# Layer 0's value projection moved out of the attention and into one stretch of seven half-size products

## The chip, the cores and the metric

The kernel runs on one core of a Trainium2 chip. The metric is the device time of one execution in microseconds. Of the kernel before, three runs were timed: 2423.89, 2424.85 and 2425.2 us, median 2424.85.

## What is computed

A decoder trunk of two layers on 1024 positions of width 1024, all in float32. Layer 0 is differential attention with 8 head pairs, layer 1 forgetting attention with 16 heads; each is followed by a gated MLP. Residuals go through a LayerNorm. What matters here is the beginning of layer 0:

```python
q, k, v = jnp.split(x @ w_qkv, 3, axis=-1)          # three 1024x1024x1024 products
q = apply_rotary(q.reshape(B, S, H, 2, d), cos, sin, PARTIAL_ROT)
k = apply_rotary(k.reshape(B, S, H, 2, d), cos, sin, PARTIAL_ROT)
v = v.reshape(B, S, H, 2 * d)
s = jnp.einsum('bhcqd,bhckd->bhcqk', qb, k) * scale
p = masked_softmax(s, causal_mask(start, Q_BLOCK, S))
a = p[:, :, 0] - lam * p[:, :, 1]
o = jnp.einsum('bhqk,bhkd->bqhd', a, v)             # then RMS norm and the output product
```

## The kernel before, in words

Every float32 operand of a large product is held as two parts, a rounded high part and a low rest (`split`, L85: ScalarE makes the high part, VectorE the rest). A product is then three matmuls (`mm3`, L97): high by high, low by high, high by low. A "step" of a projection is one such triple, 128x128 stationary by 512 columns.

Layer 0's attention goes by 8 pairs of heads (`attention`, L853). A pair has 16 jobs: 8 blocks of 128 queries, two halves each. A job is its scores on TensorE (`scores`, L647: two matmuls per up to 512 keys), the mask and row minimum in one VectorE instruction (L664), the exponential with row sums on ScalarE (L687), a reciprocal and, for the first half, the scaling of the probabilities on VectorE (L690, L692), for the second half the difference of the two on VectorE (L697). Differences are transposed on TensorE (L1531), split from PSUM into `pt` (L88, L92) and multiplied with the values (L1554). Each of these comes one job after the one before, so that the engines overlap; each engine works through its instructions in order.

While a pair attends, TensorE also projects the next one: `project` (L554) is a generator whose steps are placed between the jobs. In layer 0 these are 48 steps, for three weight slabs (queries, keys, values) of 512 KB by two halves of the positions; `attention` spreads them by weights, query block number plus 1 plus `W_C`. Work that follows a step is queued by a count of steps (`after`, L295; `pulse`, L303): copying a result to SBUF (`result`, L592, after `D_EV`), collecting the rows that rotary turns with 12 small DMAs (`gather`, L612), turning them with three VectorE instructions and four DMAs back (`turn`, L625, after `D_ROT`), splitting queries and keys (`halves`, L604, after `D_CUT`). Values come out of their projection as 128 dimensions by 512 positions; four transposes (`turn_v`, L638) bring them into the layout for L1554, and they are split into two tiles. The next weight slabs are fetched by `ahead` and split by `ready`.

The first pair's projection runs ahead of all (`first_pair_rotary`, L336): queries and keys by halves of the positions, then its values, with the loads of x, its splits, the sine tables and the constants around it. The seven other pairs' values are made inside pairs 0 to 6.

Layer 1 makes the values of all pairs ahead of its attention in one stretch (`value_steps`, L445, run by `Steps`, L1571). It splits the 1024x1024x1024 product into halves in each dimension and computes seven half-size products in place of eight, in the order 1, 2, 5 and 6 alternating, 7, 4, 3. The operands are sums and differences of the quarters: `x1` and `x2` of the activations, `B` of the weights, made by accumulating DMAs on GpSimd's queue and by VectorE (`make`). Each product has 4 row blocks by 4 inner blocks by 3 matmuls, x stationary and weights moving, 512 columns wide; the results are gathered in `c12`, split and written to `vv` in DRAM, from where `load_values` (L549) brings a pair's two value tiles back.

Instructions marked by `keep_in_program_order` stay in the order in which the program issues them on their engine; others may be moved by the scheduler when the program is built. SyncE (SP) issues most DMAs and stops at one whose data or buffer isn't ready; GpSimd (POOL) issues the rotary tables' and the accumulating ones.

## Time and profile before

| | |
|---|---|
| median of three runs | 2424.85 us |
| the profiled execution | 2425.8 us, its span 2424.0 us |
| TensorE clock granted | 0.999 |
| TensorE busy | 2388.8 us (99%), 11691 matmuls |
| VectorE busy | 1921.5 us (79%) |
| ScalarE busy | 1323.3 us (55%) |
| GpSimd busy | 160.1 us (7%) |
| layer 0's eight pairs | from 48.3 to 488.5 us |
| layer 1's eight pairs | from 1308.1 to 1719.2 us |

Busy times are of the span. A matmul's duration in the profile holds its passage through the array, in which the next one already runs; so the sum of durations is more than the time that matmuls take, and the distance between two starts is the measure. A row of a group tells, after the bar, the group's busy time, the mean duration of one in ns, the idle time of the engine just before them and what ended most of it.

### The profile page before, as it was taken

The page shows a single profiled execution, that of the slowest core. Times are in us where ns is not written, and L with a number is a line of the kernel's source. Part 1 is how long each engine was busy: PE and PEld are TensorE (multiplying, and loading weights), DVE is VectorE, ACT ScalarE, POOL GpSimd, SP SyncE. Part 2 cuts the span into 40 slices and gives each one's busy share as a digit, 9 for nine tenths or more (in the row PEclk, how much of TensorE's full clock was granted, in tenths as well). Part 3 has the DMA queues.
Part 4 walks back from the last instruction along what each step waited for, and adds up shares of the span by engine and source line. Part 5 has one row for each costly group of instructions (what it writes and reads, how often), then busy time and mean ns, then how long its engine had stood idle before and what let it go on. Part 6 is the DMA issues. An engine that isn't in the chain of part 4 may idle for free.

```text
span 2424.0 us, 33635 instructions
## 1 busy us (share of the span) xinstructions
PE 2388.8 (99%) x11691; PEld 1991.6 (82%) x11691; DVE 1921.5 (79%) x3755; ACT 1323.3 (55%) x2504; POOL 160.1 (7%) x341
## 2 busy tenths in 40 slices
PE   8999999999999999999999999999999999999998
PEld 6888888878888888888777888888888888888886
DVE  5788888999766767887876888789898676678977
ACT  4666666656544444444545777776565444445444
POOL 2111111110000000000220111110010000000000
PEclk9999999999999999999999999999999999999999
DMA  6232323622322224964476323335222222239751
GB/s 176 73 85 83 87 78 97 206 96 79 105 79 79 79 95 130 351 229 155 150 171 197 89 80 92 102 102 186 87 97 87 79 87 95 79 100 334 260 170 70
DMA packets 144322, 307.51 MB, mean 127 GB/s; under 512 B 27452, under 2 KB 46908, under 8 KB 144152
## 3 DMA queue, kind: packets, MB, share of 16 engines
q1 hardware_dynamic: 140472, 298.22, 38.5%
q0 software_dynamic: 3680, 7.15, 1.5%
q8 instruction: 92, 1.51, 0.3%
q14 instruction: 78, 0.64, 0.1%
HBM read 196.83 MB, written 67.57 MB: 109 GB/s over the span
## 4 chain that ended last, share of the span: by engine, by line
PE 82%; DVE 9%; DMA 4%; ACT 3%; issue 1%; SPq 1%; DVEq 0%; POOL 0%; ACTq 0%; POOLq 0%
PE m L101 20%; PE m L103 19%; PE m L102 19%; PE s L101 4%; PE s L102 4%; PE s L103 4%; PE m L1531 3%; PE s L662 3%; PE s L661 2%; PE m L1557 1%; DVE wo L92 1%; PE m L1556 1%; DMA pt<-in_wd 1%; DMA wb<-in_wd 1%; DVE oa L92 1%
## 5 line engine op out<-in xcount | busy, mean ns | idle before, releaser
L101 PE MATMUL m<-xh,wh 128*128 128x512 f32 x640 | 268.2, 419 | 10.8 <-ACT xh L88 8.9
L101 PE MATMUL m<-xh,wo 128*128 128x512 f32 x656 | 255.4, 389 | 0.9 <-DVE xl L92 0.9
L102 PE MATMUL m<-xl,wo 128*128 128x512 f32 x656 | 255.2, 389 | 0.0
L103 PE MATMUL m<-xh,wo 128*128 128x512 f32 x656 | 255.2, 389 | 0.0
L103 PE MATMUL m<-xh,wl 128*128 128x512 f32 x640 | 253.9, 397 | 0.4 <-DVE wl L92 0.4
L102 PE MATMUL m<-xl,wh 128*128 128x512 f32 x640 | 252.8, 395 | 0.4 <-DVE xl L92 0.4
L88 ACT ACTIVATE wo<-wg 128x512 fp32r<-128x512 f32 x168 | 106.3, 633 | 222.7 <-PE m L103 215.1
L664 DVE CUSTOM_DVE_ANT_0 s<-s,mask 128x128 f32<-128x128 f32 (+7 forms) x256 | 194.4, 760 | 22.6 <-PE s L662 21.5
L101 PE MATMUL m<-q,wo 128*128 128x512 f32 x472 | 184.0, 390 | 0.0
L102 PE MATMUL m<-q,wo 128*128 128x512 f32 x472 | 183.6, 389 | 0.0
L103 PE MATMUL m<-q,wo 128*128 128x512 f32 x472 | 183.6, 389 | 0.0
L88 ACT ACTIVATE pt<-m 128x512 fp32r<-128x512 f32 (+1 forms) x240 | 129.4, 554 | 83.4 <-PE m L1531 67.2
L92 DVE TENSOR_TENSOR pt<-m,pt 128x512 fp32r<-128x512 f32 (+1 forms) x240 | 148.9, 633 | 15.5 <-ACT pt L88 12.8
L88 ACT ACTIVATE wo<-t 128x512 fp32r<-128x512 f32 x132 | 82.7, 627 | 140.6 <-PE m L103 131.2
L656 POOL CAST qz<-q 64x128 fp32r<-64x128 f32 x256 | 101.0, 397 | 766.8 <-PE s L662 672.5
L101 PEld LDWEIGHTS m<-xh,wh 128*128 128x128 f32 x640 | 121.6, 190 | 31.7 <-ACT xh L88 8.9
L92 DVE TENSOR_TENSOR wo<-wg,wo 128x512 fp32r<-128x512 f32 x168 | 115.3, 688 | 37.9 <-ACT wo L88 37.1
L101 PEld LDWEIGHTS m<-xh,wo 128*128 128x128 f32 x656 | 123.2, 188 | 27.0 <-PE m L1120 1.4
L103 PEld LDWEIGHTS m<-xh,wo 128*128 128x128 f32 x656 | 123.1, 188 | 25.6
L102 PEld LDWEIGHTS m<-xl,wo 128*128 128x128 f32 x656 | 123.1, 188 | 25.4
L103 PEld LDWEIGHTS m<-xh,wl 128*128 128x128 f32 x640 | 121.0, 189 | 27.3 <-DVE wl L92 1.4
L102 PEld LDWEIGHTS m<-xl,wh 128*128 128x128 f32 x640 | 122.0, 191 | 16.9 <-DVE xl L92 0.9
(404 smaller groups left out, 6311.1 us busy)
## 6 DMA issues: line engine op xcount, KB each, us to landing
t<-in_wi SPq DMA_DIRECT2D x44, 512.0 KB
ha<-ad SPq DMA_DIRECT2D x88, 256.0 KB
wg<-in_wi SPq DMA_DIRECT2D x42, 512.0 KB
ad<-t SPq DMA_DIRECT2D x42, 512.0 KB
wst<-in_w SPq DMA_DIRECT2D x38, 512.0 KB
q<-q SPq DMA_DIRECT2D x128, 128.0 KB
pt<-in_wd SPq DMA_DIRECT2D x24, 512.0 KB
hb<-in_wd SPq DMA_DIRECT2D x44, 256.0 KB
```

Of the source, the lines that this page charges most:

```text
L88: i = nc.scalar.activation(hi, src, AF.Copy, scale=1.0 if scale is None else scale)
L92: nc.vector.tensor_tensor(lo, src, hi.bitcast(F32), op=ALU.subtract)
L101: mm(out, wh, xh, start=start, stop=False)
L102: mm(out, wh, xl, start=False, stop=False)
L103: mm(out, wl, xh, start=False, stop=stop)
L656: nc.gpsimd.tensor_copy(qz[r:r + 64, :], q[r:r + 64, qt * P:qt * P + P])
L661: nc.tensor.matmul(sb[:, ks], q[:, qt * P:qt * P + P], kd[:, ks], start=True, stop=False)
L662: nc.tensor.matmul(sb[:, ks], qz[rows], kl[rows, ks], start=False, stop=True)
L664: nc.vector.tensor_tensor_reduce(sb[:, :ln], sb[:, :ln], self.mask[:, S - ln:], 1.0, BIG, ALU.add, ALU.min, mn)
L1531: nc.tensor.transpose(tb[:, w:w + P], self.pts[q][:, kt * P:kt * P + P], k.ident)
L1556: mm(o, self.v[0][:, vs], h, start=first, stop=False)
L1557: mm(o, self.v[0][:, vs], l, start=False, stop=last)
```

## The change

1. Layer 0's values. `project` keeps layer 1 alone. `first_pair_rotary` prepares sums of quarters of x and of the value weights, straight from DRAM (`xT`, `wv0`), by plain DMAs on SP and accumulating ones on GpSimd, and runs `value_steps` for all pairs, after the queries and keys of pair 0 and ahead of its attention. Slabs of values, `turn_v` and its transposes are gone. Pairs fetch their values with `load_values`, 10 steps into the pair before.
2. The projection in the pairs (`project_rotary`) has 32 steps, for queries and keys. All pairs' generators are chained; pair 0 takes 36 steps, pair 6 takes 28. `W_C` of layer 0 is 6 in place of 2.
3. Rotation: gather per operand (6 DMAs at a time), turn 7 steps after the last projection, cut 11 steps after it. For pair 0, turn, gather and cut are hung on the steps of the value stretch (`V_ROT`, `V_GA`, `V_CUT`). The gather buffer `rt` is one half tile for all; its other half holds probabilities of the second half for the first four query blocks.
4. The scaling of the first half's probabilities (L692) is on ScalarE. The sums of squares in `diff_values` come two steps after in place of one.
5. The sines and the load of the exponentials' table after them are pinned on ScalarE, ahead of the second half of x; lambda's exponential comes after the queries and keys of pair 0, pinned. Spare tiles come from other pools.
6. A pair's output is stored in two parts; output tiles that are fetched back come from another pool.

The diff, without some of the plain renamings (buffers picked by layer, names, imports):

```diff
 AHEAD = 6
 EARLY = 2
-D_EV, D_ROT, D_CUT, D_TV = 1, (9, 10), ((16, 16), (22, 24)), 1
+D_EV, D_ROT, D_CUT = 1, (7, 7), ((11, 11), (11, 11))
+V_ROT, V_GA, V_CUT = (20, 42), 19, (31, 54)
+SHIFT = 4
 W_CUT = 3
-D_V, D_VAL = (5, 9), 10
-LAG, VLAG, W_C = 1, 0, (2, 6)
+D_VAL = 10
+LAG, VLAG, W_C = 1, 0, (6, 6)
 FL = 1
 TR = ((0, 1), (2, 3, 4), (5, 6, 7), ())
 PIN = 1
...
-        d = self.cp.tile([P, 2], F32, name="lamd")
+        d = self.lamd = self.cp.tile([P, 2], F32, name="lamd")
-        nc.scalar.activation(d, d, AF.Exp)
+    def lam_exp(self):
+        nc, d = self.nc, self.lamd
+        self.tc.keep_in_program_order(nc.scalar.activation(d, d, AF.Exp))
...
     def rope_tables(self):
         nc, q = self.nc, self.nc.gpsimd
         ang, n, cos, sin = self.angles
-        nc.scalar.activation(cos, n, AF.Sin)
-        nc.scalar.activation(sin, ang, AF.Sin)
+        for d, a in ((cos, n), (sin, ang)):
+            self.tc.keep_in_program_order(nc.scalar.activation(d, a, AF.Sin))
+        self.tc.keep_in_program_order(nc.scalar.preload_act_table_set("natural_log_exp_and_others"))
...
-    def exp_table(self):
-        nc = self.nc
-        with self.tc.tile_critical(no_gpsimd_drain=True):
-            nc.scalar.preload_act_table_set("natural_log_exp_and_others")
-            for t in self.angles[2:]:
-                nc.scalar.copy(t[:, :1], t[:, :1])
...
                 self.load_x(0, (4 * n + 2 * s,))
         self.rope_tables()
         self.load_x(1)
-        self.w[2] = self.weight(self.slabs[2])
     def first_pair_rotary(self, t):
-        dst = [self.tmp() for s in range(3)]
+        H, lo, hi = KT // 2, slice(0, 512), slice(512, 1024)
+        dst = [self.tmp() for s in range(2)]
         self.xh, self.xl = {}, {}
         with self.tc.tile_critical(no_gpsimd_drain=True):
             self.nc.scalar.preload_act_table_set("trig_and_small")
         self.rope_angles()
         self.first_loads()
         self.consts()
-        r = {}
+        self.rt = self.lp.tile([P, 1024], F32, tag="lg", name="rt")
+        self.lam()
+        pool = self.nc.gpsimd.dma_start
+        sync = lambda *a: self.tc.keep_in_program_order(self.nc.sync.dma_start(*a))
+        x, wv, B = self.i["xT"], self.i["wv0"], {}
+        tiles = [self.qp.tile([P, 1024], F32, tag="q1", name=self.nm("vw")) for _ in range(7)] + [self.tmp()]
+        x1 = [self.tmp(pool=self.wp, tag="wst", bufs=2) for _ in range(2)] + \
+            [self.tmp(pool=self.tt, tag="pt") for _ in range(2)]
+        x2 = [y[:, ns] for y in (self.tmp(pool=self.tt, tag="pt"), self.tmp(pool=self.pp, tag="p")) for ns in (lo, hi)]
+        c12 = [self.tmp(pool=self.pp, tag="p") for _ in range(4)]
+        hold = t[5:7] + [self.tp.tile([P, 1024], F32R, tag="of", name=self.nm("vs"), bufs=1)]
+        def weights(c):
+            for r, ns in ((1, lo), (2, hi)):
+                for k in range(H):
+                    B[r, c, k] = tiles[4 * c - 4 + k][:, ns]
+                    sync(B[r, c, k], wv[r * H - H + k][:, c * 512 - 512:c * 512])
+        def sums(d, *terms):
+            sync(d, x[:, terms[0][0], terms[0][1]])
+            for kt, ns in terms[1:]:
+                pool(d, x[:, kt, ns], accum_op=ALU.add)
+        weights(1)
+        for k in range(H):
+            sums(x1[k][:, lo], (k, hi), (H + k, hi))
+            sums(x2[k], (k, hi), (H + k, hi), (k, lo))
+        weights(2)
+        for k in range(H):
+            sums(x1[k][:, hi], (k, lo), (k, hi))
+        steps = self.value_steps(0, B, x1, x2, lambda k: pool(x2[k], x[:, H + k, lo], accum_op=ALU.add), c12, hold)
+        r = {"t": self.rt}
         for c in range(2):
             ps = [self.mbank() for _ in range(2)]
             for _ in zip(*[self.dense_steps(ps[s], *self.w[s], c) for s in range(2)]):
                 pass
+            for s in range(2):
+                self.result(0, 0, s, c, ps[s], dst[s], t, True)
+        self.lam_exp()
+        for c in range(2):
+            for j in range(2):
+                self.after(V_ROT[c] - V_GA, self.gather, dst, r, c, j)
+            self.after(V_ROT[c], self.turn, dst, r, c)
+            for j in range(2):
+                self.after(V_CUT[c], self.halves, dst, t, c, j)
+        steps.run(4)
+        steps.drains()
+        steps.run(-4)
+        self.ahead(2)
+        steps.run(-2)
+        self.load_values(0, 0, t)
+        self.ahead(3)
+        self.ready(2)
+        steps.run(-1)
+        self.ready(3)
+        steps.run()
+    def project_rotary(self, p, t):
+        dst, r, i = [None] * 2, {"t": self.rt}, 2 * p
+        for n, (s, c) in enumerate(((0, 0), (1, 0), (0, 1), (1, 1))):
+            if n % 2:
+                self.ahead(i + 2 + n // 2)
+                self.after(5, self.ready, i + 2 + n // 2, True)
+            if p == NP - 1 and n > 1:
+                self.out_ahead(0, n - 2)
+            ps = self.mbank()
+            yield from self.dense_steps(ps, *self.w[i + s], c)
+            if c == 0:
+                dst[s] = self.tmp()
+            self.after(D_EV, self.result, 0, p, s, c, ps, dst[s], t)
+            self.after(D_EV + (5 if n == 0 else 1), self.gather, dst, r, c, s)
+            if s == 1:
+                self.after(D_ROT[c], self.turn, dst, r, c)
+                for j in range(2):
+                    self.after(D_CUT[c][j], self.halves, dst, t, c, j)
             if c:
...
+                del self.w[i + s]
     def first_pair(self, l, t):
...
     def project(self, l, p, t):
...
+        i = 2 * p
+        for n, (s, c) in enumerate([(s, c) for s in range(2) for c in range(2)]):
+            if n % 2:
                 self.ahead(i + 2 + n // 2)
             else:
                 self.after(W_CUT, self.ready, i + 1 + n // 2, True)
-            if s == 2 - l and p == NP - 1:
+            if s and p == NP - 1:
                 self.out_ahead(l, c)
             ps = self.mbank()
             yield from self.dense_steps(ps, *self.w[i + s], c)
...
+            self.after(D_EV, self.result, l, p, s, c, ps, None, t)
             if c:
                 del self.w[i + s]
...
         sl = slice(c * 512, c * 512 + 512)
         if dst is not None:
-            self.nc.scalar.activation(dst[:, sl], ps, AF.Copy, scale=-DH ** -0.5 if s == 0 else 1.0)
+            i = self.nc.scalar.activation(dst[:, sl], ps, AF.Copy, scale=-DH ** -0.5 if s == 0 else 1.0)
+            if pin:
+                self.tc.keep_in_program_order(i)
         elif s == 0:
             if c == 0:
                 self.qlo = self.tp.tile([P, 1024], F32R, tag="t", name=self.nm("ql"))
...
-    def gather(self, dst, r, c):
-        if "t" not in r:
-            r["t"] = self.tmp()
-        t = r["t"][:, c * 512:c * 512 + 512]
-        for j, x in enumerate(dst[:2]):
...
+    def gather(self, dst, r, c, j):
+        t = r["t"][:, :512]
+        x = dst[j]
+        for h in range(2):
+            rows = 64 * j + 32 * h
+            n = slice(c * 512 + h * 256, c * 512 + h * 256 + 256)
+            self.nc.sync.dma_start(t[rows:rows + 32, :256], x[48:80, n])
+            for y in range(2):
+                self.nc.sync.dma_start(t[rows + y:rows + 32:2, 256:], x[49 - y:80:2, n])
-        t = r["t"][:, c * 512:c * 512 + 512]
+        t = r["t"][:, :512]
...
-    def turn_v(self, g, vf, va, vb):
-        tb = self.mbank()
-        for j in range(4):
-            self.nc.tensor.transpose(tb[:, j * P:j * P + P],
-                                     vf[:, (4 * g + j) * P:(4 * g + j + 1) * P], self.ident)
-        gs = slice(g * 512, g * 512 + 512)
-        self.after(D_TV, self.split, va[:, gs], vb[:, gs], tb)
...
         sb, ln, mn = self.scores(0, t[j], t[2 + j], t[4], j, qt)
         lsum = self.small(tag="ls")
         yield
-        pt = self.tmp(pool=self.pp, tag="p") if j == 0 else self.tmp() if last and qt > 2 else \
+        pt = self.tmp(pool=self.pp, tag="p") if j == 0 else self.rt[:, 512:] if qt < 4 and not (last and qt % 2) else \
+            self.tmp() if last and qt > 2 else \
             self.tmp(pool=self.wp, tag="wst", bufs=2)
         nc.scalar.activation(pt[:, :ln], sb[:, :ln], AF.Exp, bias=mn, scale=-1.0, accum_out=lsum)
         yield
         rs = self.small(tag="rs")
         nc.vector.reciprocal(rs, lsum)
         if j == 0:
-            nc.vector.tensor_scalar(pt[:, :ln], pt[:, :ln], rs, None, op0=ALU.mult)
+            nc.scalar.activation(pt[:, :ln], pt[:, :ln], AF.Copy, scale=rs)
             pr["p"] = pt
         else:
             p0 = pr["p"][:, :ln]
...
             nc.tensor.matmul(ms, self.ones, lo, start=False, stop=True)
             done.append(True)
-        self.after(1, sums)
+        self.after(2, sums)
         yield
         while not done:
             yield
...
         self.od = self.dr.tile([NP, P, 1024], F32, name=f"od{l}")
         tiles = lambda p: [self.qtile((p + l) % 2) for _ in range(7)] + \
             ([self.lp.tile([P, 1024], F32R, tag="lg", name=self.nm("kb"))] if l else [])
-        self.wo = NP * (3 - l)
-        self.slabs = [self.i[f"w{l}"][s * NP + p] for p in range(NP) for s in range(3 - l)]
+        self.wo = NP * 2
+        self.slabs = [self.i[f"w{l}"][s * NP + p] for p in range(NP) for s in range(2)]
         self.slabs += [self.i[f"wo{l}"][k] for k in range(8)]
         self.w, self.stage, self.queue = {}, {}, []
         self.ofs = {}
...
         cur = tiles(0)
         self.first_pair(l, cur) if l else self.first_pair_rotary(cur)
         live, values = [], []
+        tl = [[] for _ in range(NP)]
+        early = chain(*[self.project_rotary(p, tl[p]) for p in range(1, NP)])
         for p in range(NP):
-            nxt = tiles(p + 1) if p < NP - 1 else None
-            if nxt is not None:
-                self.fill, n = self.project(l, p + 1, nxt), 48 - 16 * l
-                if l:
-                    self.after(D_VAL, self.load_values, l, p + 1, nxt)
+            nxt = None
+            if p < NP - 1:
+                nxt = tiles(p + 1)
+                if l == 0:
+                    tl[p + 1] += nxt
+                    self.fill, n = early, 32 + SHIFT * ((p == 0) - (p == NP - 2))
+                else:
+                    self.fill, n = self.project(l, p + 1, nxt), 32
+                self.after(D_VAL, self.load_values, l, p + 1, nxt)
             else:
                 self.fill, n = self.out_early(l), 64
             jobs = (self.diff_jobs if l == 0 else self.fox_jobs)(p, cur)
...
             while done < n:
                 self.step()
                 done += 1
-            next(self.fill, None)
+            if l or p > NP - 3:
+                next(self.fill, None)
             cur = nxt
         self.fill, n = self.out_late(l), 12
         while live or values:
...
             self.fetch_o(l, 0)
             self.after(8, self.load_o, 0, None, (0,))
         else:
-            if l:
-                self.after(6, self.ready, self.wo + 1, True)
+            self.after(6, self.ready, self.wo + 1, True)
             self.after(3, self.load_o, 0, None, (1,))
             self.after(4, self.fetch_o, l, 1)
             self.after(8, self.load_o, 1)
...
     def finish(self):
         if self.end is not None and next(self.end, True):
             self.over = True
-            if self.last and self.p < NP - 1:
+            if self.l == 0 and self.c4 == 2 and self.p < NP - 1:
+                self.k.nc.sync.dma_start(self.k.od[self.p][:, :768], self.k.ofs[self.p][:, :768])
+            elif self.l == 0 and self.last and self.p < NP - 1:
+                self.k.nc.sync.dma_start(self.k.od[self.p][:, 768:], self.k.ofs.pop(self.p)[:, 768:])
+            elif self.last and self.p < NP - 1:
                 self.k.nc.sync.dma_start(self.k.od[self.p], self.k.ofs.pop(self.p))
```

83 lines of the change are left out of this document (17 added, 66 removed).

## The prediction

> **What bounds the kernel now.** I read the busy shares first, then the stretches of layer 0's attention one by one, then single instructions.
>
> ```profile
> span 2424.0 us, 33635 instructions
> PE 2388.8 (99%) x11691; PEld 1991.6 (82%) x11691; DVE 1921.5 (79%) x3755; ACT 1323.3 (55%) x2504; POOL 160.1 (7%) x341
> ```
>
> TensorE is busy nearly throughout. In the view by stretches the columns are length, then busy time and count for PE, PEld, DVE, ACT and POOL, the granted clock, the DMA share and GB/s. I cut at the first score product of each pair: the row from 48.30 is pair 0, 98.20 pair 1, 265.30 pair 4, 375.20 pair 6, 430.00 pair 7 (which carries the output projection). 1452.70 is a pair of layer 1, and 1208.90 is layer 1's own value stretch with what is mixed into it.
>
> ```profile
> 8.90:24.30 15.40, 14.77 (x47) 10.88 (x48) 12.67 (x28) 8.98 (x19) 5.28 (x10) 1.00 0.92 294
> ...
> 48.30:98.20 49.90, 48.27 (x246) 39.69 (x246) 40.07 (x101) 28.51 (x64) 5.80 (x16) 1.00 0.36 95
> 98.20:154.30 56.10, 55.19 (x305) 47.09 (x304) 47.18 (x118) 36.74 (x83) 5.51 (x16) 1.00 0.32 90
> ...
> 265.30:320.30 55.00, 55.00 (x306) 47.08 (x305) 46.04 (x114) 35.89 (x81) 7.06 (x16) 1.00 0.30 82
> ...
> 375.20:430.00 54.80, 54.80 (x306) 47.06 (x304) 47.00 (x112) 38.38 (x86) 7.19 (x16) 1.00 0.40 110
> 430.00:488.50 58.50, 57.29 (x305) 48.09 (x303) 56.23 (x130) 34.21 (x79) 6.05 (x15) 1.00 0.57 195
> ...
> 1452.70:1502.10 49.40, 49.12 (x298) 42.69 (x297) 40.68 (x107) 35.60 (x74) 6.03 (x16) 1.00 0.33 92
> 1208.90:1308.00 99.10, 98.66 (x444) 77.92 (x443) 73.96 (x129) 48.65 (x90) 15.17 (x18) 1.00 0.74 177
> ```
>
> A pair takes 55.0 us with TensorE never idle, VectorE busy for 46.04 and ScalarE for 35.89. So layer 0's attention is TensorE's, and VectorE has 55.00 - 46.04 = 9.0 us to spare in a pair. That reserve is what this change spends.
>
> A matmul's busy time isn't its price, since matmuls overlap. The starts tell the pitch:
>
> ```profile
> 24.73 0.39 PE L101 MATMUL m<-xh,wh 128*128 128x512 f32 x1
> ...
> 25.86 0.39 PE L103 MATMUL m<-xh,wl 128*128 128x512 f32 x1
> ...
> 279.08 0.60 PE L642 MATMUL m<-ident,t 128*128 128x128 f32 x4
> 279.44 0.48 PE L101 MATMUL m<-xh,wh 128*128 128x512 f32 x1
> ```
>
> Between the first two rows lie five steps (four rows between are left out): 1.13 / 5 = 0.227 us for a 512-wide matmul. Four transposes take 279.44 - 279.08 = 0.36 us, 0.09 each.
>
> **The change part by part.** *Removed from TensorE.* A slab is 2 x 8 x 3 = 48 matmuls. These groups over 0 to 470 us hold the 24 slabs of queries, keys and values, and the values' transposes:
>
> ```profile
> L101 PE MATMUL m<-xh,wh 128*128 128x512 f32 x384 | 159.0, 414 | 9.2 <-ACT xh L88 8.9 <-ACT wh L88 0.2
> ...
> L642 PE MATMUL m<-ident,t 128*128 128x128 f32 x64 | 10.1, 277 | 0.9 <-DVE pt L92 0.9
> ```
>
> 3 x 384 = 24 x 48, and a third of it is values: 384 matmuls x 0.227 = 87.2 us. 64 transposes x 0.09 = 5.8 us. Together -93.0.
>
> *Added to TensorE.* Seven products of 4 x 4 x 3 = 48 matmuls, all 512 wide: 336 x 0.227 = +76.3. The net is -16.7 us if TensorE waits nowhere more than now. All value work leaves the pairs: each loses 10.9 + 0.7 = 11.6 us, so a pair like that of 265.30 would be 43.4 us (pair 0 keeps four steps more and pair 6 four fewer, which cancel), and 76.3 us come in ahead of them.
>
> *Entry into the stretch.* Today the values' matmuls follow the last query/key matmul directly, on a weight split long before. Now ScalarE copies both results in pinned order, does the pinned exponential of lambda and only then splits the first value weight:
>
> ```profile
> 35.12 1.28 ACT L596 ACTIVATE t<-m 128x512 f32<-128x512 f32 x2 [2.35 <-PE m L103]
> 37.68 0.20 ACT L165 ACTIVATE lamd<-lamd 128x2 f32<-128x2 f32 x1 [1.28 <-DVE lamd L164]
> ```
>
> 1.28 + 0.20 and a 512-wide split of 0.6 (rather more than half the 1.06 of a 1024-wide one, shown below): TensorE stands for about 2.0 us near 35 us. Lower bound 0, if the copies come earlier; upper 4, if the weights land late. I take 2.0, as nothing else in the order can fill it.
>
> Such a hole can also cost clock. In layer 1 two waits close together were followed by matmuls at half pace:
>
> ```profile
> 1314.11 0.47 PE L662 MATMUL s<-q,qz 66*128 66x128 f32 x2 [1.50 <-DMA q<-cd]
> 1315.86 0.33 PE L661 MATMUL s<-q,q 128*128 128x128 f32 x1 [1.28 <-ACT p L835]
> ...
> 1317.70 0.54 PE L101 MATMUL m<-xh,wh 128*128 128x512 f32 x1
> ...
> 1319.64 0.63 PE L661 MATMUL s<-q,q 128*128 128x512 f32 x1
> 1320.07 0.63 PE L662 MATMUL s<-q,qz 66*128 66x512 f32 x1
> ...
> 1321.41 0.39 PE L101 MATMUL m<-xh,wh 128*128 128x512 f32 x1
> ```
>
> 0.43 us from 1319.64 to 1320.07 is nearly double 0.227, over some 3.7 us from 1317.70 to 1321.41: half of that, 1.8 us, is lost. Between 0 and 1.8 I take 0.9, since one hole of 2.0 is shorter than those two together (2.8).
>
> The Trainium skill (TensorE: Matmul & The Clock Gate, What's actually happening) says that the array falls to half rate only after a whole idle window of about 3.4 us, free-running. By that rule the 2.0 us hole costs no clock and the sum is 0.9 us lower; the rows above fell with 2.8 us of visible waits and two short products between them, so the rule doesn't settle it.
>
> *The stretch itself.* Layer 1's own stretch runs with TensorE busy 98.66 of 99.10 us and VectorE at 75%: 0.4 us of visible waits. Layer 0 takes its sums from accumulating DMAs on POOL's queue, 20 of them, and each second term waits for the first to land:
>
> ```profile
> pt<-xl POOLq DMA_DIRECT2D x6, 256.0 KB, 5.0
> ```
>
> ```profile
> 27.01 1.03 POOL L220 DMA_DIRECT2D rope<-rs  x2 [4.69 <-DMA rs<-sp]
> ```
>
> At 5.0 us a landing (a median, layer 1) plus issues of about half a microsecond (1.03 for two), a step k needs 6 to 7 us, the four of them 24 to 28. POOL is in the rotation tables' DMAs until 28 us; so the sums are done by 52 to 56, and the fifth product, their first reader, starts near 35 + 2 + 2 x 10.9 = 59. The bytes that products 5 and 6 need are 16 weight quarters and 20 terms of sums of 256 KB, 9 MB; at the 294 GB/s of the first row (0.92 share) they take 31 us from about 24, done by 55. Both fit, narrowly; I add 0.5, with bounds 0 and 10.
>
> *The pairs.* VectorE and ScalarE lose and gain these (pair 4, then the same scaling on ScalarE in layer 1):
>
> ```profile
> L92 DVE TENSOR_TENSOR wl<-wst,wh 128x1024 fp32r<-128x1024 f32 x3 | 3.7, 1224 | 0.6 <-ACT wh L88 0.5
> ...
> L692 DVE TENSOR_SCALAR p<-p,rs 128x128 f32<-128x128 f32 (+7 forms) x8 | 4.2, 519 | 0.2
> L690 DVE RECIPROCAL rs<-ls 128x1 f32<-128x1 f32 x16 | 2.4, 158 | 4.9 <-ACT wst L687 2.8 <-ACT p L687 2.1
> ...
> L92 DVE TENSOR_TENSOR q<-m,q 128x512 fp32r<-128x512 f32 x2 | 1.4, 692 | 0.2
> ```
>
> ```profile
> L88 ACT ACTIVATE wh<-wst 128x1024 fp32r<-128x1024 f32 x3 | 3.2, 1057 | 0.0
> L596 ACT ACTIVATE t<-m 128x512 f32<-128x512 f32 x6 | 3.6, 596 | 2.3 <-PE m L103 2.2
> L88 ACT ACTIVATE q<-m 128x512 fp32r<-128x512 f32 x2 | 1.2, 599 | 0.9 <-PE m L642 0.9
> ...
> L842 ACT ACTIVATE p<-p,rs 128x128 f32<-128x128 f32 (+5 forms) x6 | 4.4, 728 | 0.8 <-DVE rs L838 0.8
> L842 ACT ACTIVATE t<-t,rs 128x512 f32<-128x512 f32 (+1 forms) x2 | 1.9, 938 | 0.3 <-DVE rs L838 0.2
> ```
>
> VectorE: 46.0 - 1.2 (one weight) - 4.2 (scaling of the first half's probabilities) - 1.4 (values) = 39.2, 90% of 43.4. ScalarE: 35.9 - 1.1 - 1.2 - 1.2 + 6.3 = 38.7, 89%. Three engines near 90% wait on each other in turn: score, minimum on VectorE, exponential on ScalarE, reciprocal on VectorE, scaling now on ScalarE. The best likeness is pair 7 of today: VectorE at 56.23 of 58.50, 96%, and TensorE idle for only 1.2 us. Layer 1's pair with VectorE at 82% loses 0.3. So a pair's waits lie between 0.3 and 1.2 by these rows, and above that if ScalarE's 89%, which no pair has today (at most 38.38 of 54.80), costs its own. I take 0.8 x 7 = +5.6. Later sums of squares (two steps instead of one) and the other spread of steps over the jobs work on these waits and are in that number.
>
> *Pair 7* loses VectorE's scaling too, some 4 of its 56 us; of its 1.2 us idle I take 0.7 back. *Handover into pair 0*: the last products' drains stand ahead of its first scores on both engines, +1.0 (pair 0 today: 49.90 - 48.27 = 1.6 idle already).
>
> *Costed at nothing.* These rows bear on it:
>
> ```profile
> L226 ACT ACT_TABLE_LOAD x1 | 1.3, 1283 | 3.9 <-DMA t<-t 3.9
> ```
>
> ```profile
> 19.13 1.16 ACT L88 ACTIVATE xh<-p 128x512 fp32r<-128x512 f32 x2 [1.49 <-DMA p<-in_xT]
> ...
> 36.35 2.44 SPq L636 DMA_DIRECT2D t<-t  x4
> ...
> 39.82 1.14 ACT L88 ACTIVATE q<-t 128x512 fp32r<-128x512 f32 x2
> ```
>
> The table load (1.28 us) moves ahead on ScalarE, to before the splits of the second half of x; there ScalarE stands 1.49 us for the load of x anyway, which hides it; without that cover it costs 1.3 once. Rotation: turn and cut come 4 steps apart, 4 x 43.4 / 32 = 5.4 us. From the first write-back's issue to the cut that reads it passed 39.82 - 36.35 = 3.5 us, and the three VectorE operations before it, of half the size of the 692 ns subtraction above, are under 2.1: it just fits. Without that cover ScalarE waits in order at the cut, twice a pair, and the exponentials queue behind it. The gathers are issued 6 at a time instead of 12. Two value loads replace one weight load on SP's queue, and the split output store is one issue more; DMA (share 0.30 in pair 4) has room for both.
>
> **Sum.** 2425.8 (the profiled execution; its span is 2424.0) - 16.7 + 2.0 + 0.9 + 0.5 + 5.6 - 0.7 + 1.0 = 2418.4. The median of the runs is 2424.85, 0.95 under the profiled one: 2417.5. Where today's pairs 0 to 2 lose more than the later ones (pair 1: 56.10 against 55.00), the spread of steps may give back some 1.5 us: I forecast **2416**.
>
> **The rivals.**
>
> *In-order chain (slower).* VectorE and ScalarE become the bound of the pairs. VectorE's 9.0 us idle in a pair is largely waiting (4.9 at the reciprocal alone). If this waiting doesn't shrink as the pair does, a pair takes 39.2 + 9.0 = 48.2. All else gives -16.7 + 3.4 + 0.3 - 1.5 = -14.5, or 2.1 a pair: the change turns into a loss once a pair exceeds 45.5, that is, once more than 6.3 of the 9.0 us stay. At 7.2 it is 46.4 and 7 x 3.0 - 14.5 = +6.5: **2431**. For it: ScalarE at 89%, and one more trip between the two engines per job. Against it: pair 7 leaves VectorE only 2.3 us.
>
> The Trainium skill (TensorE: Matmul & The Clock Gate, the table at its head) calls ScalarE's and VectorE's queues strict first-in-first-out, eight deep. That rule speaks for this rival, since whatever waits at the head holds the rest; the reciprocal's row above shows such a wait.
>
> *Starved stretch (no change).* Sums or weights land late, as POOL's chain takes 28 us or more beside saturated DMA: each of the first steps of products 5 and 6 waits 2 to 3 us, +9 in all with the lost clock: **2425**. For it: the narrow fit above. Against: the first reader is 24 us behind the start.
>
> *Nearly the whole gain.* The engines absorb all, the hole at the entry is short, pairs 1 and 7 recover: -16.7 + 2 - 3 = **2407**.
>
> *The rotation is too close (the pinning doesn't serve).* Each of 14 cuts holds ScalarE for 1.5 us, of which half reaches TensorE: +10, **2426**.
>
> **How the numbers follow.** Forecast 0.47 (its own range 2410 to 2421), nearly the whole gain 0.14, in-order chain 0.21, starved stretch 0.11, close rotation 0.07. Changes within 0.2% (4.85 us) can't be told from none here. Faster: 0.47 less its upper end (0.03), 0.14 and a little of the last two: 0.61. Slower: the chain's 0.21 less 0.03, and the tails of the last two, 0.03: 0.21. Same: 0.18. The range for 8 in 10 runs from 2404 (all of the gain and 4 back) to 2433 (a pair at 46.5).
>
> **What will show it.** The first value product starts 2 us after the last query/key matmul; the stretch then lasts 77 to 78 us; pairs last 44 to 45 us with VectorE and ScalarE at 39 each. Wrong if pairs exceed 45.5, with TensorE waiting at the transposes for VectorE's L697 or at products for ScalarE's splits; or if products 5 and 6 wait for accumulating DMAs.

## The result, and the profile after

The changed kernel takes 2443.2 us (median of 6 runs, 2440.29 to 2446.06), the kernel before 2424.77 (6 runs beside them): ratio 1.0074, 95% interval 1.0062 to 1.0087. It is 18 us slower where I forecast 9 us faster. The profiled execution has a span of 2441.2 us, 17.2 more than before.

The head of the page, kernel after:

```profile
span 2441.2 us, 33686 instructions
...
PE 2382.1 (98%) x11579; PEld 1980.4 (81%) x11579; DVE 1919.7 (79%) x3755; ACT 1368.6 (56%) x2598; POOL 170.7 (7%) x361
```

TensorE has less to do (2382.1 us of busy time against 2388.8), as the change intends, and the time is longer all the same: it stands somewhere. The view by stretches of the kernel after says where (columns as in the prediction: length; busy time and count of PE, PEld, DVE, ACT, POOL; granted clock; DMA share; GB/s). The rows up to 137.90 are the value stretch, then come pair 0, pairs 3 and 4, 6 and 7:

```profile
24.30:35.20 10.90, 10.81 (x48) 8.63 (x46) 0.61 (x4) 1.22 (x3) 0.47 (x1) 1.00 1.03 319
35.20:50.00 14.80, 13.37 (x57) 10.81 (x58) 7.48 (x13) 6.62 (x14) 5.35 (x6) 1.00 1.00 274
50.00:60.00 10.00, 3.79 (x17) 2.82 (x15) 2.08 (x3) 1.38 (x3) 3.38 (x4) 0.84 1.11 261
60.00:70.00 10.00, 2.76 (x7) 2.19 (x8) 4.63 (x9) 0.00 (x0) 4.57 (x6) 0.50 0.91 146
70.00:80.00 10.00, 5.94 (x25) 4.60 (x24) 4.93 (x9) 2.13 (x4) 1.40 (x3) 0.97 0.68 145
80.00:90.00 10.00, 8.62 (x27) 6.09 (x26) 8.65 (x16) 5.83 (x11) 5.44 (x4) 0.66 0.92 227
90.00:137.90 47.90, 47.88 (x209) 38.51 (x208) 32.93 (x52) 27.13 (x49) 1.75 (x2) 1.00 0.62 166
137.90:179.10 41.20, 40.45 (x211) 33.86 (x210) 32.38 (x87) 31.09 (x68) 5.96 (x16) 1.00 0.52 151
266.40:310.40 44.00, 43.59 (x249) 37.48 (x249) 38.69 (x103) 36.36 (x85) 5.40 (x16) 1.00 0.41 114
310.40:355.20 44.80, 43.74 (x250) 37.35 (x248) 39.36 (x104) 37.10 (x86) 5.10 (x16) 1.00 0.40 112
399.70:448.90 49.20, 46.20 (x261) 38.31 (x261) 44.16 (x115) 41.23 (x95) 5.81 (x16) 1.00 0.56 165
448.90:502.90 54.00, 51.92 (x268) 43.07 (x269) 48.35 (x113) 32.34 (x74) 4.07 (x15) 1.00 0.55 177
```

The pairs came out as forecast: 44.0 and 44.8 us where 55.0 stood. The value stretch did not: from 50 to 70 us TensorE works 6.5 of 20 us. Four places of it, kernel after, TensorE's instructions with the idle time before them in brackets:

```profile
36.41 0.50 PE L104 MATMUL s<-wo,xh 128*128 128x512 f32 x1 [1.30 <-ACT wo L91]
...
67.24 0.80 PE L105 MATMUL m<-wo,xh 128*128 128x512 f32 x1 [13.45 <-DVE wo L95]
...
79.68 0.50 PE L104 MATMUL m<-wo,q 128*128 128x512 f32 x1 [4.06 <-DVE p L512]
83.11 1.22 PE L104 MATMUL s<-wo,q 128*128 128x512 f32 x2 [1.38 <-ACT wo L91]
```

The first is the entry. The second is the loss: TensorE waits 13.45 us for the low part of a weight (L95) of the second product. What VectorE did in that time, kernel after:

```profile
54.02 0.69 DVE L512 TENSOR_TENSOR t<-t 128x512 f32<-128x512 f32 x1 [1.48 <-DMA t<-in_wv]
64.17 0.43 DVE L663 TENSOR_TENSOR rt<-rt,rope 128x256 f32<-128x256 f32 x1 [9.46 <-DMA rt<-t]
65.69 0.43 DVE L662 TENSOR_TENSOR rt<-rt,rope 128x256 f32<-128x256 f32 x1 [1.09 <-DMA bf<-in_bf]
66.15 0.42 DVE L664 TENSOR_TENSOR rt<-rt 128x256 f32<-128x256 f32 x1
66.50 1.29 DVE L95 TENSOR_TENSOR wo<-vw,wo 128x512 fp32r<-128x512 f32 x2
...
77.39 0.43 DVE L663 TENSOR_TENSOR rt<-rt,rope 128x256 f32<-128x256 f32 x1 [4.53 <-DMA rt<-t]
```

VectorE stood at pair 0's first turn (L662 to L664), 9.46 us for the gathered rows, and the weight split that TensorE wanted came next on it. At 77.39 the second turn did the same for 4.53 us. The gathers came late on SP's queue, kernel after:

```profile
42.80 1.51 SPq L348 DMA_DIRECT2D wst<-in_xT  x2
...
49.18 0.62 SPq L653 DMA_DIRECT2D rt<-t  x1
...
60.94 1.22 SPq L655 DMA_DIRECT2D rt<-t  x2
```

The first gather is issued at 49.18, behind the loads of weights and of the sums' first terms (L348), the last two in the row of 60.94: the twelve of this half go out over some 12 us. And the DMA engines are full. Their use from 35 to 75 us by queues (packets, MB, share of 16 engines), kernel after:

```profile
q0 software_dynamic: 2304, 4.20, 62.2%
q1 hardware_dynamic: 3320, 4.90, 37.9%
```

The two queues together take 100% of the 16 engines for 40 us. q0 is POOL's, the accumulating transfers. They cost 62.2% of 40 us for 4.20 MB, 5.9 us a MB; the plain ones 37.9% of 40 us for 4.90 MB, 3.1 us a MB. An accumulated byte takes nearly twice the DMA time of a plain one.

The budget, in us (profiled executions; the forecast's terms regrouped, the changed kernel of experiment 8 beside it):

| part | forecast | after | experiment 8 |
|---|---|---|---|
| first value product to pair 0's first score | 78.5 | 101.5 | 83.2 |
| pairs 0 to 5, against 326.9 before | -63.6 | -65.1 | -64.3 |
| pairs 6 and 7, against 113.3 before | -14.2 | -10.1 | -7.1 |
| behind pair 7 | 0 | +2.8 | 0.0 |

78.5 is the middle of the prediction's 77 to 78 and its handover of 1.0. The 23.0 us too many in the first row are the last three rows of TensorE above, 13.45 + 4.06 + 1.38 = 18.9 us of idle, and some 4 us of half clock after them (60 to 90 us hold 7, 25 and 27 matmuls in 2.76, 5.94 and 8.62 us of busy time; at 0.227 us each that is 13.4 of 17.3). The border between pair 7 and what follows isn't sharp, since steps of the output projection stand on both sides of it; from pair 6's start to the end of the program the kernel after gains 7.3 us (2041.5 against 2048.8 before) and experiment 8 gains 7.1 (2041.7).

### The profile page after: what moved, and what is told of

The parts are those of the page before. It is cut to its first block, busy times and chain, and to the rows that moved or that the text cites. A ratio compares the mean times of both kernels' runs of the same rounds, so it can differ in the third digit from the quotient of the medians.

```text
span 2441.2 us, 33686 instructions
## 1 busy us (share of the span) xinstructions
PE 2382.1 (98%) x11579; PEld 1980.4 (81%) x11579; DVE 1919.7 (79%) x3755; ACT 1368.6 (56%) x2598; POOL 170.7 (7%) x361
## 4 chain that ended last, share of the span: by engine, by line
PE 77%; DVE 9%; DMA 6%; ACT 5%; issue 2%; SPq 1%; DVEq 0%; ACTq 0%
PE m L104 18%; PE m L106 18%; PE m L105 18%; PE s L104 5%; PE s L105 5%; PE s L106 5%; PE m L1561 3%; PE s L685 2%; PE s L684 2%; PE m L1587 1%; PE m L1586 1%; DVE wo L95 1%; DMA pt<-in_wd 1%; DMA pt<-in_xT 1%; DVE s L687 1%
## 5 line engine op out<-in xcount | busy, mean ns | idle before, releaser
L104 PE MATMUL m<-xh,wh 128*128 128x512 f32 x512 | 219.1, 428 | 10.6 <-ACT xh L91 8.8
L106 PE MATMUL m<-xh,wl 128*128 128x512 f32 x512 | 203.5, 398 | 0.0
L105 PE MATMUL m<-xl,wh 128*128 128x512 f32 x512 | 202.7, 396 | 0.5 <-DVE xl L95 0.5
L95 DVE TENSOR_TENSOR pt<-m,pt 128x512 fp32r<-128x512 f32 (+1 forms) x240 | 148.5, 632 | 18.3 <-ACT pt L91 15.2
L679 POOL CAST qz<-q 64x128 fp32r<-64x128 f32 x256 | 94.1, 370 | 730.9 <-PE s L685 607.5
L95 DVE TENSOR_TENSOR wo<-wg,wo 128x512 fp32r<-128x512 f32 x168 | 115.3, 687 | 37.5 <-ACT wo L91 36.5
L684 PE MATMUL s<-q,q 128*128 128x512 f32 (+3 forms) x384 | 131.9, 344 | 5.2 <-DMA q<-q 1.7
L91 ACT ACTIVATE oa<-ha 128x512 fp32r<-128x512 f32 x108 | 67.3, 628 | 118.0 <-PE s L106 54.2
L95 DVE TENSOR_TENSOR wo<-t,wo 128x512 fp32r<-128x512 f32 x134 | 92.2, 688 | 45.2 <-ACT wo L91 45.1
```

The costliest lines, as they stand in the source:

```text
L91: i = nc.scalar.activation(hi, src, AF.Copy, scale=1.0 if scale is None else scale)
L95: nc.vector.tensor_tensor(lo, src, hi.bitcast(F32), op=ALU.subtract)
L104: mm(out, wh, xh, start=start, stop=False)
L105: mm(out, wh, xl, start=False, stop=False)
L106: mm(out, wl, xh, start=False, stop=stop)
L679: nc.gpsimd.tensor_copy(qz[r:r + 64, :], q[r:r + 64, qt * P:qt * P + P])
```

## The experiments

My theory from here on: VectorE stands, in order, at pair 0's turn, whose gathers are late because they pass through DMA engines filled by the weights and the accumulated sums. The rival: the sums or weights themselves are late, and the turn only happens to stand where the wait shows. Line numbers move by one to three in the experiments. Spans of time are those of the profiled executions.

**1. The turn later.**

```diff
-V_ROT, V_GA, V_CUT = (20, 42), 19, (31, 54)
+V_ROT, V_GA, V_CUT = (64, 84), 19, (75, 95)
```

> The changed kernel with pair 0's rotation moved back in the value stretch: turns 64 and 84 steps in (20 and 42 in the change), gathers 19 steps before them, cuts at 75 and 95. In the changed kernel TensorE loses 31.3 us up to pair 0's first score at 137.9 us, of which some 8 are the start of the program; the largest wait (13.6 us, ending at 67.24) ends when VectorE splits a weight, and VectorE had stood 9.5 us at the turn. Theory A, VectorE stands in order at the turn behind gathers that come late out of a full DMA queue, and the splits of the second product's weights stand behind it: without the early turn about 20 of those us go, pair 0 starts at 117 to 120, the total is 2422 to 2426. Theory B, the sums and weights themselves are late and the turn only shows it: TensorE waits nearly as long at the second, fifth or sixth product, pair 0 starts at 132 or later, the total is 2437 or more.

2442.98 us (4 runs), ratio 1.0069, 1.0053 to 1.0086: no change against the kernel after. TensorE in the kernel of experiment 1:

```profile
68.14 0.79 PE L105 MATMUL m<-wo,xh 128*128 128x512 f32 x1 [14.25 <-DVE wo L95]
```

The edit did not do what it says: in the built program the turn's three instructions still stand between the weight differences and the second product's splits on VectorE, as in the kernel after. The turn isn't pinned, and the scheduler put it ahead of the second product's splits whichever step issued it. So this run says nothing on the theory, and shows what the step numbers were worth.

**2. The late turn with early gathers.** As 1, but the first half's gathers at step 1, where the kernel after has them too, and the second half's behind the first turn.

```diff
-                self.after(V_ROT[c] - V_GA, self.gather, dst, r, c, j)
+                self.after((1, V_ROT[0] + 1)[c], self.gather, dst, r, c, j)
```

> As the run with the late turn, but the gather of the first half stays where the change has it (one step into the stretch); only the turns and cuts are late. Theory A1, the turn's place in VectorE's order is what costs: same as the late turn, 2422 to 2426. Theory A2, the gathers' place on SyncE's queue and in the DMA queues, ahead of weights or sums, is what costs: most of the loss stays, 2435 or more.

2439.47 us (4 runs), ratio 1.0061, 1.0046 to 1.0076; pair 0 starts at 134.3 instead of 137.9. TensorE in the kernel of experiment 2:

```profile
66.00 0.80 PE L105 MATMUL m<-wo,xh 128*128 128x512 f32 x1 [11.51 <-DVE wo L95]
```

The wait is 1.9 us shorter than in the kernel after. The time lies where the expectation puts a loss by the gathers' place, but the run doesn't show that: it moved nothing either. SP issues the first gather at 48.06 here, at 50.14 in experiment 1 and at 49.18 in the kernel after, each time behind the same loads, and VectorE has the turn ahead of the splits in all three.

**3. Without the accumulating transfers.** Left out are 16 of the 20, so that sums keep their first term alone and the values are other numbers; the work of the engines stays.

```diff
             sync(d, x[:, terms[0][0], terms[0][1]])
-            for kt, ns in terms[1:]:
-                pool(d, x[:, kt, ns], accum_op=ALU.add)
```

> The changed kernel without the 16 accumulating DMAs of the sums ahead of the stretch: each sum is its first term alone, so the values come from wrong operands; all TensorE, VectorE and ScalarE work stays. 4 of 11 MB are not moved. If the full DMA queue makes the gathers late, VectorE's wait at the first turn (9.5 us, TensorE's 13.6) shrinks to below 5 and pair 0 starts by 127 us, total 2425 to 2433. If SyncE's own issue order makes them late, the first gather is issued near 49 us as now and pair 0 starts at 134 or later, total 2438 or more.

2431.53 us (one run), within the expected range; pair 0 starts at 127.7, 0.7 us later than expected. TensorE in the kernel of experiment 3:

```profile
55.88 0.50 PE L105 MATMUL m<-wo,xh 128*128 128x512 f32 x1 [2.06 <-DVE wo L95]
...
68.12 0.79 PE L104 MATMUL m<-wo,q 128*128 128x512 f32 x1 [3.71 <-DVE p L510]
```

And VectorE there, at the second turn:

```profile
65.84 0.42 DVE L661 TENSOR_TENSOR rt<-rt,rope 128x256 f32<-128x256 f32 x1 [4.67 <-DMA rt<-t]
```

The instruction that waited 13.45 us waits 2.06. No accumulated sum is an operand of that matmul or of the split before it. So late sums aren't the cause, and the DMA time that the accumulating transfers take is part of it; whether it is late gathers or late weights that stop TensorE is left to experiments 5 and 8. From its first gather to its last, SP now takes 7.2 us (44.99 to 52.19) where it took 12.4 (49.18 to 61.57). The second turn is another matter: VectorE stands 4.67 us there against 4.53 in the kernel after, and TensorE behind it 3.71 against 4.06. That wait doesn't come from the accumulating transfers. The second half's gathers are issued behind the first turn's write-backs, over 7.1 us in both kernels.

**4. The scaling back on VectorE.** This asks whether the pairs are bound by the engines beside TensorE (the in-order rival of the prediction).

```diff
-            nc.scalar.activation(pt[:, :ln], pt[:, :ln], AF.Copy, scale=rs)
+            nc.vector.tensor_scalar(pt[:, :ln], pt[:, :ln], rs, None, op0=ALU.mult)
```

> The changed kernel with the scaling of the first half's probabilities back on VectorE. Pairs 1 to 5 last 43.5 to 44.8 us now, with VectorE busy for 38.5 and ScalarE for 36.2. If VectorE's share sets the pairs once it passes some 95%, it would be busy for 42 to 43 of 44 and the pairs grow to 45 to 46.5: total 2451 to 2460. If TensorE bounds them all the same, pairs stay within 0.5 us and the total within 4 of the changed kernel's 2443.

2449.13 us (one run). Kernel of experiment 4, a stretch of a pair's length:

```profile
266.40:310.40 44.00, 43.64 (x248) 37.09 (x248) 41.26 (x111) 31.78 (x77) 6.88 (x16) 1.00 0.41 114
```

VectorE is at 41.26 of 44.00 us (94%) and pairs 2 to 5 still take 44.1 us: even there TensorE sets the pair. Neither expectation holds as a whole, though: the time lies 5.9 us above the kernel after, between the two ranges. Pairs 1 (47.6) and 7 (59.2) grew, pairs 0 (39.7) and 6 (44.9) shrank; the eight together take 367.9 us against 365.0 in the kernel after. I did not follow what made pairs 1 and 7 longer.

**5. The turn later, and pinned.** As 1, and pair 0's gathers and turns keep their program order on SP and VectorE.

```diff
-        nc.vector.tensor_tensor(r2, r2, self.sin[:, cs], op=ALU.mult)
-        nc.vector.tensor_tensor(r1, r1, self.cos[:, cs], op=ALU.mult)
-        nc.vector.tensor_tensor(r2, r2, r1, op=ALU.add)
+        keep = self.tc.keep_in_program_order if pin else (lambda i: i)
+        keep(nc.vector.tensor_tensor(r2, r2, self.sin[:, cs], op=ALU.mult))
+        keep(nc.vector.tensor_tensor(r1, r1, self.cos[:, cs], op=ALU.mult))
+        keep(nc.vector.tensor_tensor(r2, r2, r1, op=ALU.add))
...
-            self.after(V_ROT[c], self.turn, dst, r, c)
+            self.after(V_ROT[c], self.turn, dst, r, c, True)
```

> The late turn again, now with pair 0's gathers and turns kept in program order on SyncE and VectorE. In the run with the late turn the built order on VectorE was the same as in the changed kernel: the turn's three instructions stand 57th to 59th, between the weight differences (L512) and the second product's last two splits, since the scheduler takes their data as landed and moves them ahead. So that run moved nothing, and theory A is untested. Here the splits come right after the differences. Theory A: the 13.6 us wait shrinks to 1 or 2, pair 0 starts at 116 to 121 us, the total is 2421 to 2427. Theory B (sums or weights late by themselves): the wait moves on to the fifth and sixth product, pair 0 starts at 130 or later, the total is 2436 or more.

2424.77 us (10 runs), ratio 0.9999, 0.999 to 1.0009; pair 0 starts at 119.6. Both as expected. The 13.45 us are gone, and 18 us of the time with them, while every byte still moves, so the second product's weights were there in time (its low parts come right behind the last weight difference, which ends at 51.04): TensorE is busy without a break from 55 to 70 us, with the DMA engines as full as before. The gathers moved too, though: the first is issued at 65.34, behind the full stretch, so this run doesn't tell the turn's place from the gathers'. Experiment 8 does. Two stretches of the kernel of experiment 5, in the columns of above:

```profile
55.00:70.00 15.00, 15.00 (x68) 12.39 (x67) 14.65 (x24) 8.89 (x16) 5.24 (x6) 1.00 1.09 243
...
109.15:115.00 5.85, 5.57 (x16) 4.20 (x17) 5.10 (x8) 3.45 (x6) 0.00 (x0) 0.71 0.92 269
```

What is left is another wait at the end of the stretch, on ScalarE and then on TensorE:

```profile
106.35 1.22 ACT L91 ACTIVATE q<-t 128x512 fp32r<-128x512 f32 x2 [3.49 <-DMA t<-rt]
```

```profile
109.15 0.73 PE L104 MATMUL m<-wo,q 128*128 128x512 f32 x2 [3.73 <-ACT wo L91]
```

ScalarE stands 3.49 us at pair 0's second cut for the write-back of the turn 11 steps earlier, the split of the last product's weights stands behind it, and TensorE waits 3.73 us and runs at clock 0.71 afterwards.

**6. Pinned at the old places.** The pinning of 5 with `V_ROT` (20, 42) as in the change.

> The changed kernel's own places (turns 20 and 42 steps in) with gathers and turns kept in program order. The first turn then stands among the second product's splits rather than ahead of them. If only the scheduler's moving ahead costs, this is as good as the late one: pair 0 at 116 to 121 us. If step 20 is too soon for the gathers by itself (they land at 64 to 66 us, and step 20 comes 14 us after 37), most of the wait stays: pair 0 at 128 to 138, total 2433 to 2443.

2440.26 us (one run), within the expected range; pair 0 at 140.1, 2 us beyond it. TensorE in the kernel of experiment 6:

```profile
65.22 0.79 PE L105 MATMUL m<-wo,xh 128*128 128x512 f32 x1 [10.72 <-DVE wo L95]
```

Step 20 itself is too early: the cure in 5 is the later place, and the pinning only makes the place hold. Experiments 1, 5 and 6 together show it: 1 lacks the pinning, 6 the place, and 5 has both.

**7. The output's splits pinned too.** As 5, and the splits of the first two fetched output tiles (`load_o`) pinned on ScalarE, against the waits in pairs 6 and 7.

```diff
-            self.split(self.oh[k, c], self.ol[k, c], src[:, c * 512:c * 512 + 512])
+            self.split(self.oh[k, c], self.ol[k, c], src[:, c * 512:c * 512 + 512], pin=k < 2)
```

> As the late pinned turn, and the splits of the first two fetched output tiles (load_o) on ScalarE kept in program order too. In the changed kernel ScalarE stands 2.8 us in pair 6 at such a split, for a fetch issued only 4 us before, and VectorE 1.9 us behind it; pair 6 lasts 49.2 us with 28 steps. If that is the same fault, pair 6 falls to 45 to 47 us and the total is 2 to 4 us below the late pinned run: 2418 to 2424. If pair 6 is long because ScalarE is full (41 of 49 us), nothing changes.

2433.29 us (6 runs), ratio 1.0027, 1.0015 to 1.0039. A miss, 8.5 us above experiment 5: ScalarE no longer stands 3.13 us at such a split in pair 6, as it does in 5, but pair 6 stays at 49.7 us (49.4 in 5), and in pair 7, which grows to 58.8, ScalarE stands 4.83 us for a fetch. The order of these splits isn't the cause of pair 6's length.

**8. The turn in the middle, the cut far behind it.** The pinning of 5 with

```diff
-V_ROT, V_GA, V_CUT = (20, 42), 19, (31, 54)
+V_ROT, V_GA, V_CUT = (46, 66), 19, (66, 86)
```

> The turn with pair 0's gathers and turns pinned as in e5, but at steps 46 and 66 of the value stretch with the cuts 20 steps behind each (66 and 86), so that nothing is asked of the gathers soon and ScalarE meets no cut whose write-back has just been issued. Theory (two separate waits: VectorE in order at pair 0's first turn, cured in e5; ScalarE in order at pair 0's second cut, 3.9 us at 109.15 in e5 plus half clock behind it): the hole near 109 goes, pair 0 starts at 113 to 116 instead of 119.6, and the time is 2418 to 2421, faster than the kernel before. Rival (the ScalarE hole of e5 belongs to the drains of the last products, not to the cut): pair 0 again at 119 to 120 and 2424 to 2426, no change against before.

2421.28 us (11 runs, 2418.36 to 2425.23), ratio 0.9985, 0.9976 to 0.9994: the best kernel here, 22 us faster than the change and 3.4 faster than before, though by less than the 0.2% of a clear difference. It is 0.3 us above the expected range, and pair 0 starts at 118.5, not by 116. The hole of 109 is gone, as the theory said; a smaller one stands elsewhere. Kernel of experiment 8, the first half's gathers on SP's queue:

```profile
48.68 0.62 SPq L654 DMA_DIRECT2D rt<-t  x1
...
60.37 1.22 SPq L656 DMA_DIRECT2D rt<-t  x2
```

They go out when they did in the kernel after (49.18 to 60.94), into DMA engines as full, and TensorE's 13.45 us at the second product are 1.79 all the same. What differs up to there is the turn's place on VectorE: it stands at 71.57, behind the splits. This is what experiment 5 left open.

The same kernel by stretches and on TensorE:

```profile
50.00:55.00 5.00, 3.21 (x14) 2.29 (x14) 3.04 (x6) 0.31 (x1) 1.76 (x2) 0.97 1.10 274
55.00:60.00 5.00, 5.00 (x17) 4.01 (x16) 4.32 (x8) 0.97 (x2) 1.74 (x2) 0.69 1.10 239
```

```profile
54.51 0.63 PE L105 MATMUL m<-wo,xh 128*128 128x512 f32 x1 [1.79 <-DVE wo L95]
...
57.49 0.63 PE L106 MATMUL m<-wo,xl 128*128 128x512 f32 x1
57.92 0.50 PE L104 MATMUL m<-wo,xh 128*128 128x512 f32 x1
...
431.00 0.30 PE L686 MATMUL s<-q,q 128*128 128x128 f32 x1 [2.08 <-DMA rt<-t]
```

The split of the second product's weights is 1.79 us late even without the turn, since it stands behind the weight differences, whose loads are in the same full DMA engines. The half clock behind it, eight matmuls from 54.51 to 57.92 in 3.41 us instead of 8 x 0.227 = 1.82, costs 1.6 more. In the profiled execution of experiment 10, with the same stretch, TensorE works all of 50 to 60 us, so this wait doesn't come every time.

**9. The same number of steps for every pair.** As 8, with 32 steps in all pairs.

```diff
-SHIFT = 4
+SHIFT = 0
```

> As e8, but every pair of layer 0 gets 32 steps of projection (SHIFT 0; the change gives pair 0 36 and pair 6 28). Theory (pairs 6 and 7 fall some 4 us short of the forecast because pair 6, with four steps fewer, has too little projection between its scores): pair 6 grows by less than pair 0 shrinks (2.7 us of TensorE work move), and the time is 2 to 4 us below that of e8. Rival (the shortfall comes from the output projection's loads and splits, which queue in pairs 6 and 7 however the steps are spread): pairs 0 and 6 change by the same 2.7 us with opposite signs, and the time is that of e8 within 1.5 us.

2447.91 us (4 runs), ratio 1.0098, 1.0084 to 1.0112: both expectations missed, by 26 us. Pairs 1 to 5 grow from 43.4 to 44.3 us to between 47.7 and 50.7. Kernel of experiment 9, pair 1's first score:

```profile
161.46 0.30 PE L686 MATMUL s<-q,q 128*128 128x128 f32 x1 [1.88 <-DMA q<-q]
```

Pair 0's four extra steps are a lead on which all the pairs live: without it the queries and keys of pair 1 are still being written back when the pair begins. In pairs 2 to 5 the loss is spread over small waits, which I did not follow. For pairs 6 and 7 the run settles nothing.

**10. The lead kept to the end.** As 8; pair 6's 28 steps are handed out as if they were 32.

```diff
-                    self.fill, n = early, 32 + SHIFT * ((p == 0) - (p == NP - 2))
+                    self.fill, n = early, 32 + SHIFT * (p == 0)
```

> As e8, but pair 6's 28 steps of projection are handed out as if they were 32, so that they end four steps before its jobs do and pair 7 keeps the lead of four steps that the other pairs have. Theory (part of what pairs 6 and 7 fall short of the forecast is pair 7's first score, which in e8 waits 2.2 us at 431.0 for the transfers of queries and keys made just before it, because the lead ends with pair 6): that wait goes, pairs 6 and 7 together shrink from 106.2 to 103 to 105 us, and the time is 2418 to 2420. Rival (without projection between its last jobs pair 6 loses the same time to waits between the engines): the wait at pair 7's start goes, but others of 2 us or more come in pair 6's last quarter; 106 to 108 us for the two pairs and 2421 to 2423.

2424.72 us (11 runs, 2421.25 to 2428.94), ratio 0.9999, 0.9989 to 1.0008. Kernel of experiment 10, pairs 6 and 7, then TensorE:

```profile
383.30:429.00 45.70, 42.49 (x244) 36.36 (x245) 40.48 (x108) 39.18 (x92) 6.55 (x16) 1.00 0.52 156
429.00:486.70 57.70, 56.37 (x288) 45.65 (x288) 52.46 (x121) 34.77 (x78) 5.49 (x15) 1.00 0.55 183
```

```profile
424.65 0.51 PE L686 MATMUL s<-q,q 128*128 128x512 f32 x1 [1.57 <-ACT wst L713]
...
427.88 0.39 PE L105 MATMUL m<-pt,q 128*128 128x256 f32 x1 [0.89 <-DVE pt L95]
```

The two pairs take 103.4 us, within the theory's range, and the wait of 2.08 at pair 7's start is gone; but two waits have come in pair 6's last quarter, as the rival said (1.57 and 0.89, not 2 or more), and the median is above the rival's range. In this execution pair 0 (44.6) and pair 3 (45.2) are longer than in 8 (42.7 and 44.0), where the edit reaches nothing. What pairs 6 and 7 gained is no gain: from pair 6's start to the end of the program it is 2041.7 us in both (2425.0 - 383.3 here, 2422.8 - 381.1 in 8), so it only stands behind pair 7 instead.

## Why the prediction was wrong

**The step that failed is "the stretch itself", +0.5 with bounds 0 and 10.** It cost 23.0 us more than forecast. Two things are in it.

*The DMA time of accumulated bytes.* I divided 9 MB by 294 GB/s, the rate of plain loads, and took 31 us. From 35 to 75 us an accumulated MB took 5.9 us against 3.1, so the engines are full to about 70 us (0.91 from 60 to 70), not to 55. By these prices my 9 MB, a third of them accumulated, take some 36 us (an estimate). Nor were the sums done by 52 to 56: the twelve accumulating transfers that products 5 and 6 need are issued from 37.34 to 63.91. Experiment 3 takes away the bytes with their price, so it doesn't tell the double price from the mere load. This could be read before: layer 1's own stretch, kernel before, 1195 to 1235 us, has

```profile
q1 hardware_dynamic: 3563, 6.95, 52.2%
q0 software_dynamic: 887, 1.61, 24.1%
```

7.5% for a plain MB and 15.0% for an accumulated one, the same factor of two. I looked at landings and issues of these transfers, not at what they took of the engines.

*Who waits for it.* Under "costed at nothing" I checked only that turn and cut are 4 steps apart within the pairs, and mentioned the smaller gathers. I did not ask what stands behind pair 0's turn on VectorE when its gathers share the engines with 9 MB. Experiments 3, 5 and 8 show this wait as the cause: with less DMA load the same matmul waits 2.06 instead of 13.45 us, and with the turn moved behind the splits and pinned there the wait is gone (5) or 1.79 us (8, gathers at their old time) with the load unchanged. The second turn's part, 4.06 us of TensorE, is the same wait in order on VectorE, but without the accumulating transfers as its reason (3.71 in experiment 3). The "starved stretch" rival (2425) had the place and the DMA pressure, but another victim (the sums of products 5 and 6) and less than half the price; no matmul of those products waited for an accumulating transfer in the trace.

The Trainium skill (TensorE: Matmul & The Clock Gate, the table at its head) says that VectorE's queue is strictly first in, first out. The trace agrees: the last weight difference ended at 54.71, and the split that TensorE waited for stood behind the turn until 66.50. I used this rule for the pairs, where it cost nothing, and not for the stretch, where it cost everything.

**Net TensorE work, -16.7: right.** The six pairs 0 to 5 lost 65.1 us, forecast 63.6.

**Entry, +2.0: right.** 1.30 us of idle for ScalarE's split; by the starts of the matmuls, over 0.227 us each, 1.96 us are lost there and before the next matmul.

**Half clock after the entry, +0.9: it did not come** (granted clock 1.00 from 35.20 to 50.00). The Trainium skill (TensorE: Matmul & The Clock Gate, What's actually happening) wants a whole idle window of about 3.4 us, free-running, before the clock falls; that fits this hole. It doesn't fit experiment 8, where a wait of 1.79 us with unbroken matmuls before it was followed by half clock for 3.41 us. By the starts of the matmuls that hole is 1.95 us, as large as the entry's 1.96; one cost nothing more and one 1.6 us. Nor did half clock follow the wait of 2.08 us at 431.00 in experiment 8. My bounds of 0 and 1.8 held both.

**The pairs, +0.8 each: right, and VectorE at 38.7 and ScalarE at 36.4 us in pair 3** (forecast 39.2 and 38.7). The in-order rival needed pairs above 45.5 and gets 43.5 to 44.8; experiment 4 adds that VectorE at 94% still doesn't bind them.

**The close rotation** (rival, 2426) didn't show in the pairs. It is real for pair 0 once the larger wait is gone: experiment 5 has ScalarE standing 3.49 us at the second cut, and 20 steps instead of 11 remove it.

**Pairs 6 and 7, -14.2: 4 us too much.** Pair 6 with four steps fewer was to shrink to 41; it takes 49.2, and pair 7 54.0 in place of 57.8, as work moves between them. In the kernel after, ScalarE and TensorE:

```profile
410.81 0.63 ACT L91 ACTIVATE xh<-t 128x512 fp32r<-128x512 f32 x1 [2.82 <-DMA t<-od]
```

```profile
412.69 0.55 PE L1561 MATMUL m<-ident,p 128*128 128x128 f32 x3 [1.08 <-DVE pt L95]
...
448.90 0.30 PE L684 MATMUL s<-q,q 128*128 128x128 f32 x1 [1.11 <-DMA q<-q]
...
473.79 0.50 PE L104 MATMUL m<-wh,xh 128*128 128x512 f32 x1 [1.22 <-DVE acc L1020]
```

The fetch of an output tile, the last queries and keys, and the residual's loads each come a microsecond late, 3.4 us in all, since the pairs have become shorter and these transfers have not. The order of the splits (7), the spread of the steps (9) and the lead (10) did not give them back; a version that fetches them earlier wasn't tried.

**Behind pair 7, 0: +2.8** in the kernel after, +0.7 in experiment 5 and 0.0 in 8, with the same code. In the kernel after, some 1.7 of it, by estimate, is half clock near 1260 us (granted clock 0.57 over the 4 us from 1258). Taken together with pairs 6 and 7 the gain is 7.3 us here and 7.1 in experiments 8 and 10, of 14.2 forecast.

With the turn moved, the change is worth -1.2 us in the profiled execution of experiment 8: pair 0 starts 70.2 us later (118.5 against 48.3), pairs 0 to 5 give back 64.3 and pairs 6 and 7 another 7.1. By the medians it is -3.4. What is missing from the forecast lies in the value stretch (4.7 over) and in pairs 6 and 7 (7.1 short).

## What to carry to other kernels

When work is moved to where the DMA engines are full, list every instruction there that reads a small transfer, and ask what stands behind it on its in-order engine: here three VectorE instructions of 0.4 us held back TensorE for 13 us. Count also the time that issuing such transfers takes: the second half's twelve gathers took 7 us of it. Price an accumulating transfer by its queue's share of the engines for each MB in the trace, not by the rate of plain loads. A place given by a count of steps holds only if the instruction is pinned, and pinning alone at a bad place is no better; look at the order on the engine after building, before reading the place off the source.
